# Two column blocks in one pass, splits ordered behind shifts, and stores moved to one queue, in a hybrid mixer and expert layer

## The chip, the cores and the metric

One core of a Trainium2 chip runs the whole layer. The metric is the device time of one execution in microseconds (us); lower is better. The engines are named as follows: TensorE (PE in the rows; PEld is its weight load), VectorE (DVE), ScalarE (ACT), GpSimd (POOL) and SyncE (SP, which here only issues DMAs).

## What is computed

One layer on 512 tokens of width 1024. A mixing sublayer projects x once, `p = h @ w_in`, and three mixers share the columns: trailing-window pooling, RWKV-7 (with a delta-rule state, and small "lora" projections for decay and gate), and a chunked mLSTM. Then an output projection, a norm, and an expert layer with 4 of 32 experts a token:

```python
p = h @ w_in[l]
y_pool, y_rwkv, y_mlstm = pool_mixer(p_pool), rwkv7_mixer(p_rwkv), mlstm_mixer(p_mlstm)
mix = jnp.concatenate([y_pool, y_rwkv, y_mlstm], axis=-1) @ w_out[l]
h = layer_norm(DEEPNORM_ALPHA * h + mix, ln1_g[l], ln1_b[l])
ffn = moe_ffn(h, router_w[l], router_b[l], w_gate_up[l], ...)
h = layer_norm(DEEPNORM_ALPHA * h + ffn, ln2_g[l], ln2_b[l])
```

In `rwkv7_mixer` the lora part is `w_log = -softplus(-(w0 + tanh(wd) @ w2)) - 0.5` and `g = sigmoid(gd) @ g2`, on columns that were first mixed with those of the token before (the token shift).

## The kernel before, in words

**Products in split form.** Every matmul of the mixing stage with x or a weight splits each operand into a high part (`xhi`, `whi`, made by ScalarE) and the rest (`xlo`, `wlo`, made by VectorE or GpSimd from the raw tile and the high part), lines 170 to 173. A product is then three matmuls: high by high, high by low, low by high (lines 222 to 224). x, transposed, comes as eight tiles of 128 x 512. A block of 128 columns of `w_in` comes as two tiles of 128 x 512 (four k each), through two raw buffers (`wraw`), four `whi` and four `wlo` (line 1590), so a raw buffer is free again when the low half has been made.

**The front.** `load_x` (183) loads x and the first block; `rwkv_lora` (511) takes the blocks of `ORDER` from the start: 1408 (decay and rate: `wdad`) and 1536 (gate: `gd`). `inproj_T` (213) takes a block from the queue of loaded ones, calls for the load of the next one, and does its 24 matmuls in a bank of tag `pi` (two banks; `ps` has four, `pm` two). `shift_mix` (505) evicts: ScalarE scales (507), VectorE adds the shifted columns (508). The tanhs follow (523, 525), and the lora matmul (566) needs the first of them. Then `rwkv_prep` runs k, r and v of the first heads, with transposes (`flip`, 606).

**The jam.** `rwkv_base` (674) inverts 32 x 32 blocks in a chain of 62 small VectorE operations (699, 701), whose result `xb` is stored to memory by four DMAs, two on SyncE, two on ScalarE (703), loaded back in another layout (704, `bb<-xd`) and transposed by VectorE (705). Beside this, TensorE does the mLSTM's v and o columns (`ml_vo`, 249 to 251), ScalarE evicts them (258, 259), and two last blocks of q and k follow (`ml_qk`, blocks 4 and 5, called "qk" below): evicted by 287, three taps on VectorE (289, `cv`), tanh 290, product 291 (`ks`). `rwkv_base_out` (712) places the blocks (`XT`, `X`: 728, 730, 733), with memsets on GpSimd (735); `rwkv_inv` (746) joins them to 128 x 128 inverses in steps over four chunks: 762 with puts 763, 768 with puts 769, 773 with X on ScalarE (774), 779, 784, 789. Score matmuls of the mLSTM (373) lie between. GpSimd works on `Vt` (844, 848), then makes the low halves of the `w_out` tiles, whose first four go through the same `wraw` buffers (`out_weights`, 869; load 877).

**Order.** The kernel is written in one order, and a scheduler orders the instructions of each engine from it before the run; each engine then runs its own list strictly in that order. `self.after(a, b)` only tells the scheduler to place a behind b.

## Time and profile before

| what | us |
|---|---|
| median of 3 runs (1463.05 to 1465.02) | 1463.57 |
| the profiled execution | 1465.28 |
| its span in the trace | 1463.5 |
| TensorE busy | 1334.6 (91%) |
| VectorE, ScalarE, GpSimd busy | 448.4, 289.5, 206.8 |
| DMA engines, mean rate over the span | 316 GB/s |

The page's rate by slices of 36.6 us goes from 253 GB/s in the first slice (x and the first weights) down to some 50 to 140 in the mixing stage, and from the twelfth slice on it stays near 400 until the end of the expert stage. The first matmul of the experts (line 1285) starts at 379.73. In a row of a timeline the first number is the start in us from the span's start, the second the length; "x5" groups neighbours; what stands in brackets is how long the engine had been idle and what released it. A released-by of "issue" names nothing that the trace shows; the engine's own queue is then where to look.

### The profile page before, as it was taken

The numbers are of one execution on the slowest core, as the hardware profiler recorded it, in microseconds if no ns is written. First come the engines' busy times: TensorE is split into PE (matmuls) and PEld (weight loads), VectorE is DVE, ScalarE is ACT, GpSimd is POOL, SyncE is SP. The second block draws the span as 40 slices with busy tenths as digits, with TensorE's granted clock in tenths as the row PEclk, the third lists the DMA queues.
The fourth block names the chain that finished last, engine by engine and source line by source line (L and its number), as shares of the span: only waits on it lengthen the run. The fifth ranks groups of instructions, "written<-read, shape, count | busy, mean of one in ns | idle before, by whom it ended". The sixth has DMA issues, their size and how long they took to land. (4 is left out here: it accounts for less than half of the span.)

```text
span 1463.5 us, 19946 instructions
## 1 busy us (share of the span) xinstructions
PE 1334.6 (91%) x7860; PEld 623.9 (43%) x7861; DVE 448.4 (31%) x1070; ACT 289.5 (20%) x617; POOL 206.8 (14%) x190
## 2 busy tenths in 40 slices
PE   7899978998999999987899999999879878899995
PEld 5677878876533333322233333333323222333323
DVE  5767687788521112111111121111111111211114
ACT  4444342453011111110001111111100100111103
POOL 1211236241001100110001111011100100010100
PEclk9999996899999999999999999999999999999998
DMA  7222233346899999999999999999999999999974
GB/s 253 73 58 72 52 79 99 132 141 269 297 364 375 396 385 403 396 390 395 403 403 397 396 398 399 406 394 394 391 389 402 394 404 395 400 395 415 408 297 118
DMA packets 95232, 461.88 MB, mean 316 GB/s; under 512 B 18084, under 2 KB 26692, under 8 KB 45962
## 3 DMA queue, kind: packets, MB, share of 16 engines
q1 hardware_dynamic: 79962, 435.61, 75.9%
q0 software_dynamic: 10592, 20.49, 6.5%
q10 hardware_dynamic: 4560, 4.15, 0.9%
q8 instruction: 82, 1.34, 0.4%
q14 instruction: 36, 0.29, 0.1%
HBM read 445.97 MB, written 18.10 MB: 317 GB/s over the span
## 5 line engine op out<-in xcount | busy, mean ns | idle before, releaser
L1285 PE MATMUL gu<-wc,xT 128*64 128x512 f32 x2048 | 486.5, 603 | 65.1 <-DMA wc<-w_gate_up 62.2
L1285 PEld LDWEIGHTS gu<-wc,xT 128*64 128x64 f32 x2048 | 143.1, 137 | 388.5 <-issue 243.1
L1298 DVE TENSOR_SCALAR glu<-gu 128x256 f32<-128x256 f32 (+1 forms) x64 | 35.6, 556 | 829.1 <-PE gu L1290 376.6
L1331 PE MATMUL dn<-wc,aT 128*64 128x512 f32 x1024 | 247.5, 603 | 4.2 <-PEq L1278 2.4
L1299 ACT ACTIVATE glu<-glu 128x256 f32<-128x256 f32 (+1 forms) x64 | 33.5, 524 | 543.1 <-DVE glu L1298 543.1
L1217 POOL DMA_INDIRECT xg<-hd,gidx x31 | 30.9, 998 | 670.8 <-PE tr L1230 660.8
L1331 PEld LDWEIGHTS dn<-wc,aT 128*64 128x64 f32 x1024 | 65.1, 136 | 118.9 <-issue 102.3
L1290 PE MATMUL gu<-wc,xT 128*32 128x512 f32 x960 | 111.5, 596 | 0.0
L1336 POOL DMA_INDIRECT yd<-eo,sidx x45 | 70.1, 1557 | 275.2 <-ACT eo L1335 275.2
L222 PE MATMUL pi<-xhi,whi 128*128 128x512 f32 x152 | 65.0, 428 | 15.9 <-ACT whi L172 8.9
L1231 ACT ACTIVATE xT<-tr 128x384 f32<-128x384 f32 x62 | 29.8, 490 | 181.1 <-PE tr L1230 181.1
L223 PE MATMUL pi<-xlo,whi 128*128 128x512 f32 x152 | 63.7, 419 | 0.5 <-DVE xlo L173 0.5
L224 PE MATMUL pi<-xhi,wlo 128*128 128x512 f32 x152 | 62.8, 413 | 0.0
L1290 PEld LDWEIGHTS gu<-wc,xT 128*32 128x32 f32 x960 | 27.0, 109 | 80.1 <-issue 79.8
L1335 ACT ACTIVATE eo<-dn,gate 128x512 f32<-128x512 f32 (+1 forms) x45 | 27.9, 621 | 163.0 <-PE dn L1331 88.9
L1326 PE MATMUL dn<-wc,aT 128*32 128x256 f32 x960 | 56.1, 381 | 1.0 <-ACT aT L1313 1.0
L173 POOL TENSOR_TENSOR wlo<-wraw,whi 128x512 fp32r<-128x512 f32 (+1 forms) x28 | 39.0, 1397 | 124.3 <-ACT whi L172 120.3
L1326 PEld LDWEIGHTS dn<-wc,aT 128*32 128x32 f32 x960 | 29.5, 110 | 34.0 <-issue 14.6
L172 ACT ACTIVATE whi<-wraw 128x512 fp32r<-128x512 f32 (+1 forms) x54 | 33.8, 634 | 47.8 <-DMA wraw<-w_in 21.9
L222 PEld LDWEIGHTS pi<-xhi,whi 128*128 128x128 f32 x152 | 30.0, 197 | 26.2 <-ACT whi L172 8.5
L1301 DVE SCALAR_TENSOR_TENSOR glu<-glu 128x256 f32<-128x256 f32 (+1 forms) x64 | 35.4, 555 | 7.2 <-ACT glu L1299 6.2
L1312 PEld LDWEIGHTS tr<-ident,glu 128*128 128x128 f32 x192 | 25.5, 208 | 26.4 <-DVE sel L1237 19.5
(489 smaller groups left out, 1501.1 us busy)
## 6 DMA issues: line engine op xcount, KB each, us to landing
wc<-w_gate_up SPq DMA_DIRECT2D x256, 1024.0 KB
wc<-w_down SPq DMA_DIRECT2D x128, 1024.0 KB
wraw<-w_in SPq DMA_DIRECT2D x46, 256.0 KB
wraw<-w_out SPq DMA_DIRECT2D x16, 256.0 KB
xraw<-xT SPq DMA_DIRECT2D x4, 512.0 KB
res<-x SPq DMA_DIRECT2D x4, 512.0 KB
hd<-res ACTq DMA_DIRECT2D x4, 512.0 KB
res<-yd POOLq DMA_DIRECT2D x4, 512.0 KB
```

The source lines that it names most:

```text
L172: self.hi_ins = nc.scalar.activation(hi, src, AF.Copy)
L173: return (eng or nc.vector).tensor_tensor(lo, src, hi, OP.subtract)
L222: nc.tensor.matmul(p, hi, xh, start=(k == 0), stop=False)
L223: nc.tensor.matmul(p, hi, xl, start=False, stop=False)
L224: nc.tensor.matmul(p, lo, xh, start=False, stop=(k == NK - 1))
L1285: mm(p[q][64 * h:64 * h + 64], xT[:, k, 0:64], w[:, 1024 * q + 512 * h:1024 * q + 512 * h + 512], start=False, stop=(k == NK - 1))
L1290: self.nc.tensor.matmul(p[2][32 * c:32 * c + 32], xT[:, k, 64:96], w4[:, c], start=False, stop=(k == NK - 1), skip_group_check=True)
L1298: nc.vector.tensor_scalar(out[:, c], g, 7.0, None, OP.min)
L1301: nc.vector.scalar_tensor_tensor(out[:, c], ln[:, c], 1.0, out[:, c], OP.add, OP.mult)
L1326: mm(p2[32 * c:32 * c + 32], aT[:, 4 + k % 2, 32 * (k // 2):32 * (k // 2) + 32], wd[k][:, 256 * c:256 * c + 256], start=(k == 0), stop=(k ...
L1331: mm(p0[64 * h:64 * h + 64], aT[:, k % 4, 64 * (k // 4):64 * (k // 4) + 64], wd[k][:, 512 * h:512 * h + 512], start=(k == 0), stop=(k == N ...
L1336: return nc.gpsimd.indirect_dma_start(out=self.yd.rearrange("t (c f) -> (t c) f", f=w), out_offset=bass.IndirectOffsetOnAxis(ap=self.sidx[ ...
```

## The change

It has these parts.

1. `load_x`: 20 matmuls on a zeroed tile (`idle`) into a bank of `pm` ahead of all others; the first two column blocks are loaded tile by tile between the tiles of x, first halves of both, then second halves (their low halves on VectorE; the second halves' raw buffers are those of the first).
2. `inproj_two`, new: both blocks in one pass over k, in banks of tag `ps` instead of `pi`. `rwkv_lora` calls it, shifts both, and only then loads the fourth block (the one behind the third, which `inproj_two` itself calls for), with its splits placed behind the scaling of the second shift. The tanhs come behind.
3. `rwkv_base`: the four stores of the inverted blocks are all issued by SyncE.
4. Three small casts of VectorE (`trib`, `sel0`) are placed behind the low half of the last of the first four tiles.

```diff
@@ -185,13 +185,39 @@
         self.xhi = [self.slot("x", f"xhi{q}", F32R)[:, :2048].rearrange("p (k t) -> p k t", k=4) for q in range(2)]
         self.xlo = [self.slot("yz"[q], f"xlo{q}", F32R)[:, :2048].rearrange("p (k t) -> p k t", k=4) for q in range(2)]
         xs = [self.slot("tu"[q], f"xraw{q}")[:, :2048].rearrange("p (k t) -> p k t", k=4) for q in range(2)]
-        for q in range(0, NK, 2):
-            nc.sync.dma_start(xs[q // 4][:, q % 4:q % 4 + 2], self.a["xT"][128 * q:128 * q + 256].rearrange("(k p) t -> p k t", p=128))
-            if q == 0:
-                self.wq, self.at = deque(), 0
-                self.load_next()
-        for k in range(NK):
-            self.split(xs[k // 4][:, k % 4], self.xhi[k // 4][:, k % 4], self.xlo[k // 4][:, k % 4], nc.gpsimd if k in (3, 6) else None)
+        z = self.slot("k", "idle", BF)[:, 0:512]
+        nc.vector.memset(z, 0.0)
+        p = self.bank("pm")
+        for _ in range(20):
+            nc.tensor.matmul(p, z[:, 0:128], z, start=True, stop=True)
+        x2 = lambda k, n: nc.sync.dma_start(xs[k // 4][:, k % 4:k % 4 + n], self.a["xT"][128 * k:128 * (k + n)].rearrange("(k p) t -> p k t", p=128))
+        sx = lambda k: self.split(xs[k // 4][:, k % 4], self.xhi[k // 4][:, k % 4], self.xlo[k // 4][:, k % 4], nc.gpsimd if k in (3, 6) else None)
+        self.wq, self.at, w, self.w_ins = deque(), 2, [[], []], []
+
+        def load(b, q):
+            raw, hi, lo = self.wtiles(4, 128)
+            c0 = ORDER[b][0]
+            nc.sync.dma_start(raw, self.a["w_in"][:, NK * c0:NK * (c0 + 128)].rearrange("p (k c) -> p k c", k=NK)[:, q:q + 4])
+            w[b] += [(hi[:, k], lo[:, k]) for k in range(4)]
+            return raw, hi, lo
+
+        x2(0, 1)
+        w0 = load(0, 0)
+        x2(1, 1)
+        w1 = load(1, 0)
+        for k in (2, 4, 6):
+            x2(k, 2)
+        sx(0)
+        self.split(*w0)
+        sx(1)
+        self.split(*w1)
+        sx(2)
+        sx(3)
+        self.split(*load(0, 4))
+        self.start_lo = self.split(*load(1, 4))
+        for k in range(4, NK):
+            sx(k)
+        self.wq.extend((ORDER[b][0], w[b]) for b in range(2))
 
     def load_w(self, c0, n, m, eng=None):
         src = self.a["w_in"][:, NK * c0:NK * (c0 + n)].rearrange("p (k c) -> p k c", k=NK)
@@ -200,6 +226,7 @@
             raw, hi, lo = self.wtiles(m, n)
             self.nc.sync.dma_start(raw, src[:, q:q + m])
             self.split(raw, hi, lo, eng)
+            self.w_ins.append(self.hi_ins)
             out += [(hi[:, k], lo[:, k]) for k in range(m)]
         return out
 
@@ -223,6 +250,20 @@
             nc.tensor.matmul(p, hi, xl, start=False, stop=False)
             nc.tensor.matmul(p, lo, xh, start=False, stop=(k == NK - 1))
         return p
+
+
+    def inproj_two(self):
+        nc = self.nc
+        w = [self.wq.popleft()[1] for _ in range(2)]
+        self.load_next()
+        ps = [self.bank("ps") for _ in range(2)]
+        for k in range(NK):
+            xh, xl = self.xhi[k // 4][:, k % 4], self.xlo[k // 4][:, k % 4]
+            for p, (hi, lo) in zip(ps, (z[k] for z in w)):
+                nc.tensor.matmul(p, hi, xh, start=(k == 0), stop=False)
+                nc.tensor.matmul(p, hi, xl, start=False, stop=False)
+                nc.tensor.matmul(p, lo, xh, start=False, stop=(k == NK - 1))
+        return ps
 
 
     def ml_vo(self):
@@ -519,9 +560,14 @@
         self.one = self.sp.tile([128, 4, 129], BF, name="one")
         nc.gpsimd.memset(self.one, 1.0)
         nc.gpsimd.memset(self.one[:, :, 0:1], 0.0)
-        self.after(self.shift_mix(self.inproj_T(1408), 9, self.wdad), self.hi_ins)
+        p0, p1 = self.inproj_two()
+        self.shift_mix(p0, 9, self.wdad)
+        first = self.shift_mix(p1, 10, self.gd)
+        self.w_ins = []
+        self.load_next()
+        for d in self.w_ins:
+            self.after(d, first)
         nc.scalar.activation(self.wdad[0:64], self.wdad[0:64], AF.Tanh)
-        self.shift_mix(self.inproj_T(1536), 10, self.gd)
         nc.scalar.activation(self.gd, self.gd, AF.Tanh, scale=0.5)
         nc.vector.tensor_scalar(self.gd, self.gd, 0.5, 0.5, OP.mult, OP.add)
         sr = [self.slot("r", f"R{q}") for q in range(2)]
@@ -700,7 +746,7 @@
                                     mb[:, t, t + 1:].unsqueeze(1).to_broadcast([96, t + 1, 31 - t]), OP.mult)
             nc.vector.tensor_tensor(xb[:, 0:t + 1, t + 1:], xb[:, 0:t + 1, t + 1:], v, OP.add)
         for q in range(4):
-            (nc.scalar if q % 2 else nc.sync).dma_start(quad(xd)[q], xb[24 * q:24 * q + 24])
+            nc.sync.dma_start(quad(xd)[q], xb[24 * q:24 * q + 24])
         nc.sync.dma_start(xtc, xd)
         nc.vector.transpose(sb[:, 1280:2048], sb[:, 512:1280])
         self.base_out, self.ys = (xtc, xc), sb[:, 0:512]
@@ -1152,7 +1198,7 @@
         self.onesb = self.cp.tile([128, 128], BF, name="onesb")
         nc.gpsimd.memset(self.onesb, 1.0)
         self.trib = self.cp.tile([128, 128], BF, name="trib")
-        nc.vector.tensor_copy(self.trib, c["mask2"][:, 0:128])
+        self.after(nc.vector.tensor_copy(self.trib, c["mask2"][:, 0:128]), self.start_lo)
         self.mkb = self.cp.tile([128, NT, NE], BF, name="mkb")
         self.sel0 = self.expert_sel(0)
         self.ro = self.cp.tile([128, 3, NT, 4], F32, name="ro")
@@ -1233,8 +1279,12 @@
 
     def expert_sel(self, e):
         sel = self.mw.tile([128, 2, 128], F32R, name="sel") if e else self.cp.tile([128, 2, 128], F32R, name="sel0")
-        self.nc.vector.tensor_scalar(sel[:, 0], self.c["bsel0"], 2.0 * e, None, OP.is_equal)
-        self.nc.vector.tensor_scalar(sel[:, 1], self.c["bsel2"], 4.0 * e, None, OP.is_equal)
+        d = self.nc.vector.tensor_scalar(sel[:, 0], self.c["bsel0"], 2.0 * e, None, OP.is_equal)
+        if not e:
+            self.after(d, self.start_lo)
+        d = self.nc.vector.tensor_scalar(sel[:, 1], self.c["bsel2"], 4.0 * e, None, OP.is_equal)
+        if not e:
+            self.after(d, self.start_lo)
         return sel
 
 
```

Where the instructions go, at three places. The same statements have later line numbers in the changed kernel: 258 is 299 there, 287 is 328, 703 is 749, 774 is 820.

ScalarE at the end of v and o, before; `whi<-wraw` is the split of a `w_in` tile, V and so are the evictions:

```order
L256 ACTIVATE V_1543<-ps 128x4x64 x2
L172 ACTIVATE whi<-wraw 128x512 x2
L703 DMA xd<-ba 24x32x32 x2
L258 ACTIVATE V_1543<-pi 128x2x64
L259 ACTIVATE so<-pi 128x128
L258 ACTIVATE V_1543<-pi 128x2x64
L259 ACTIVATE so<-pi 128x128
L258 ACTIVATE V_1543<-pm 128x2x64
L259 ACTIVATE so<-pm 128x128
```

And now:

```order
L297 ACTIVATE V_1591<-ps 128x4x64 x2
L172 ACTIVATE whi<-wraw 128x512 x3
L299 ACTIVATE V_1591<-pi 128x2x64
L300 ACTIVATE so<-pi 128x128
L172 ACTIVATE whi<-wraw 128x512
L299 ACTIVATE V_1591<-pi 128x2x64
L300 ACTIVATE so<-pi 128x128
L299 ACTIVATE V_1591<-pm 128x2x64
L300 ACTIVATE so<-pm 128x128
```

The two stores are gone from this list; the next block's first tile is split ahead of the first eviction, and its second between the first and second pair of evictions.

ScalarE later, at the inverse, before; the `whi` here are those of the `w_out` tiles:

```order
L730 ACTIVATE XT<-bb 32x12x32 x4
L287 ACTIVATE cv<-pi,pcol 128x512
L172 ACTIVATE whi<-wraw 128x512 x2
L774 ACTIVATE X<-ps 32x6x32 x4
L903 ACTIVATE mr<-Y 128x128
L903 ACTIVATE mr<-lora 128x128
L172 ACTIVATE whi<-wraw 128x512 x2
L290 ACTIVATE cv<-cv 128x512
```

And now:

```order
L328 ACTIVATE cv<-pi,pcol 128x512
L776 ACTIVATE XT<-bb 32x12x32 x4
L331 ACTIVATE cv<-cv 128x512
L172 ACTIVATE whi<-wraw 128x512 x3
L820 ACTIVATE X<-ps 32x6x32
L172 ACTIVATE whi<-wraw 128x512
L820 ACTIVATE X<-ps 32x6x32 x3
L949 ACTIVATE mr<-Y 128x128
```

The third `w_out` tile's split now stands ahead of the first X, the fourth's ahead of the second; block five's tanh (290, now 331) has moved from behind all of them to ahead.

VectorE around the transpose of the inverted blocks, before:

```order
L173 TENSOR_TENSOR wlo<-wraw,whi 128x512
L705 STREAM_TRANSPOSE bb<-bb 128x768
L173 TENSOR_TENSOR wlo<-wraw,whi 128x512
L341 COPY cdec<-pm 128x12
L346 COPY Q<-pm 128x96
L289 SCALAR_TENSOR_TENSOR cv<-pi,pcol,cv 128x511
L289 SCALAR_TENSOR_TENSOR cv<-pi,pcol,cv 128x510
L289 SCALAR_TENSOR_TENSOR cv<-pi,pcol,cv 128x509
L728 COPY XT<-bb 32x12x32
```

And now:

```order
L382 COPY cdec<-pm 128x12
L387 COPY Q<-pm 128x96
L330 SCALAR_TENSOR_TENSOR cv<-pi,pcol,cv 128x511
L330 SCALAR_TENSOR_TENSOR cv<-pi,pcol,cv 128x510
L330 SCALAR_TENSOR_TENSOR cv<-pi,pcol,cv 128x509
L764 MEMSET X 32x24x32
L332 SCALAR_TENSOR_TENSOR ks<-cv 128x512
L330 SCALAR_TENSOR_TENSOR cv<-pi,pcol,cv 128x511
L330 SCALAR_TENSOR_TENSOR cv<-pi,pcol,cv 128x510
L330 SCALAR_TENSOR_TENSOR cv<-pi,pcol,cv 128x509
L751 STREAM_TRANSPOSE bb<-bb 128x768
L774 COPY XT<-bb 32x12x32
```

The three `cv` operations of block five have come ahead of the transpose, which were spread over the puts of line 780 before; the `ks` of block four too.

At the front, the first tanh now stands behind the two splits of block four on ScalarE, and the lora matmul (566, now 612) on TensorE behind 11 of the third block's 24 matmuls (ahead of all of them before). The flip of v (606, now 652) comes 5 matmuls later in the block that it interrupts.

## Rows read from the trace of the kernel before

**Rows 1.** Busy time, clock, DMA share, GB/s of a stretch: the expert stage.
```profile
380.00:1410.00 1030.00, 960.23 (x5470) 330.50 (x5466) 144.71 (x338) 116.19 (x236) 100.05 (x76) 1.00 1.01 393
```

**Rows 2.** Timeline, TensorE, front (start, duration, operation, [idle <- released by]).
```profile
15.16 0.45 PE L224 MATMUL pi<-xhi,wlo 128*128 128x512 f32 x1
...
23.60 0.40 PE L224 MATMUL pi<-xhi,wlo 128*128 128x512 f32 x1
23.93 1.13 PE L566 MATMUL ps<-lora 64*128 64x512 f32 x4
...
46.64 0.65 PE L606 MATMUL ps<-ident,M 128*128 128x128 f32 x4 [0.98 <-DVE M L508]
```

**Rows 3.** Timeline, VectorE, front.
```profile
11.28 5.28 DVE L173 TENSOR_TENSOR xlo<-xraw,xhi 128x512 fp32r<-128x512 f32 x5
```

**Rows 4.** Timeline, ScalarE, front.
```profile
19.95 0.63 ACT L523 ACTIVATE lora<-lora 64x512 f32<-64x512 f32 x1 [0.82 <-DVE lora L508]
20.97 0.63 ACT L172 ACTIVATE whi<-wraw 128x512 fp32r<-128x512 f32 x1 [0.40 <-DMA wraw<-w_in]
```

**Rows 5.** Timeline, ScalarE, jam.
```profile
213.76 1.02 ACTq L703 DMA_DIRECT2D xd<-ba  x2
214.83 0.28 ACT L258 ACTIVATE V<-pi 128x128 f32<-128x128 f32 x1 [6.22 <-issue]
...
238.91 0.32 ACT L774 ACTIVATE X<-ps 32x192 f32<-32x192 f32 x1 [5.39 <-PE ps L773]
...
242.99 0.32 ACT L774 ACTIVATE X<-ps 32x192 f32<-32x192 f32 x1 [1.04 <-PE ps L773]
...
245.28 0.63 ACT L172 ACTIVATE whi<-wraw 128x512 fp32r<-128x512 f32 x1 [0.76 <-DMA wraw<-w_out]
```

**Rows 6.** Timeline, TensorE, jam.
```profile
215.33 0.80 PE L222 MATMUL pi<-xhi,whi 128*128 128x512 f32 x1 [7.04 <-ACT so L259]
...
229.14 0.39 PE L224 MATMUL pi<-xhi,wlo 128*128 128x512 f32 x1
...
235.04 0.79 PE L373 MATMUL pi<-qs,ks 64*128 64x128 f32 x2 [3.77 <-DVE ks L291]
...
243.34 5.06 PE L779 MATMUL ps<-X,M 64*64 64x64 f32 x45
...
250.84 1.22 PE L373 MATMUL pi<-qs,ks 64*128 64x128 f32 x4
...
255.45 6.82 PE L789 MATMUL ps<-R,XT 128*128 128x128 f32 x35
```

**Rows 7.** Busy times by stretch (next to last three: clock, DMA share, GB/s).
```profile
214.00:216.00 2.00, 0.67 (x2) 0.57 (x3) 0.86 (x2) 1.17 (x8) 0.21 (x1) 0.50 0.67 134
```

**Rows 8.** Timeline, SyncE's queue (DMA issues).
```profile
18.23 1.03 SPq L201 DMA_DIRECT2D wraw<-w_in  x2
...
240.57 7.04 SPq L877 DMA_DIRECT2D wraw<-w_out  x4
```

**Rows 9.** Timeline, VectorE, jam.
```profile
208.44 0.68 DVE L173 TENSOR_TENSOR wlo<-wraw,whi 128x512 fp32r<-128x512 f32 x1
...
225.33 2.30 DVE L289 SCALAR_TENSOR_TENSOR cv<-pi,pcol,cv 128x511 f32<-128x511 f32 x3
227.55 0.81 DVE L728 COPY XT<-bb 32x384 f32<-32x384 f32 x1
228.47 0.70 DVE L718 MEMSET X<- 32x768 f32 x1
...
233.62 1.37 DVE L291 SCALAR_TENSOR_TENSOR ks<-cv 128x512 f32<-128x512 f32 x1
235.02 1.52 DVE L763 COPY X<-ps 32x192 f32<-32x192 f32 x4
```

**Rows 10.** Timeline, GpSimd, jam.
```profile
229.65 1.92 POOL L735 MEMSET XT<- 32x384 f32 x3 [0.93 <-PE pi L224]
...
239.28 2.48 POOL L173 TENSOR_TENSOR wlo<-wraw,whi 128x512 fp32r<-128x512 f32 x2
```

## The prediction

> **What bounds the kernel now.** I read the busy times by stretch first. From 380 to 1410 us the DMA engines are busy all the time, at 393 GB/s [rows 1]: the expert stage streams its weights. It begins when the mixing stage is over, so an edit of the mixing stage alone moves the end by what it moves that start; I take this as one for one. The change sits at two places there, and I then read both in the timeline, engine by engine.
>
> *The front, to 47 us.* TensorE starts 36 intervals between the matmuls at 15.16 and 23.60, 0.234 us each, which is the upper clock level [rows 2]. Before that VectorE sets the pace: it makes the low halves one behind the other, five of x taking 5.28 us from 11.28 up to 16.56 [rows 3]. The tanh of the first block runs at 19.95, long before the lora matmul at 23.93 needs it [rows 2, 4]. At 46.64 TensorE lost 0.98 us to the shift of v on VectorE [rows 2].
>
> *The jam, 208 to 256 us.* ScalarE wants to evict V and so, but two stores of the inverted blocks stand ahead in its queue and wait for the chain on VectorE to end; they go at 213.76 and the first eviction starts at 214.83 after 6.22 us idle [rows 5]. TensorE stands still until 215.33 [rows 6], and the granted clock is 0.50 in 214 to 216, the lower level [rows 7]. Then qk block four, block five (last matmul 229.14), the copies of the inverse, and a wait of 3.77 us at 235.04 for ks [rows 6].
>
> **The change, part by part.** *Warm-up matmuls.* Twenty on zeroed data, in a time when TensorE waits for x anyway: cost nothing; what covers them is the wait of the first real matmul for the first splits.
>
> *Two blocks together.* Both want k = 0 to 3 while the splits still run, so TensorE works inside VectorE's time. VectorE's list is x as before to 16.5, then two more w low halves at about 0.6: 17.7. What is left, k = 4 to 7 of both, is 24 matmuls, 24 x 0.234 = 5.6, and the first of them can run from 16.7: end 22.3, against 23.60 + 0.23 = 23.83 before. Gain 1.5.
>
> *Fourth block's splits behind the shifts.* The tanhs now stand on ScalarE behind two splits that wait for tiles. Before, a tile issued at 18.23 [rows 8] was split at 20.97 [rows 4]: 2.7 us. The tiles of block four can be issued only when the low halves of block three are done, about 21.4 and 22.2; they land near 24 and 25, the second split ends at 25.6, the tanh at 26.2. The lora matmul stands after 11 matmuls of block three, reached at 22.3 + 2.6 = 24.9: stall 1.3. It gives back nearly all of the 1.5: net -0.2. Five more matmuls ahead of the flip of v cover up to 0.98 of the wait at 46.64. Front: **-0.5**, ends -1.5 and +1.
>
> *All stores on SyncE.* ScalarE was idle from 208.6 (214.83 less 6.22). But block five's first split now stands ahead of the first eviction, its second ahead of the rest. The tile is issued when VectorE is through with a low half of block four, made from 208.44 for 0.68 [rows 9] and now one operation of the chain (0.35) earlier: 208.8. It lands at 211.5, split to 212.15; V and so follow; TensorE restarts at 212.6, 2.7 earlier, after 4.3 us idle instead of 7.04. If the clock holds, 24 x 0.234 makes block four end at 218.2 and block five at 224.2 instead of 229.4. SyncE issues two stores more, 1.02 as ScalarE's two took [rows 5], so the load of the inverted blocks is about that later; no matter, since ahead of the transpose now stand the second block's three cv operations, 2.30 together as the first block's [rows 9]. 224.4 + 0.8 + 2.3 = 227.5, transpose 228.4, copies of 5.4 us (227.55 to 235.02, less the memset of 0.70 and ks of 1.37, which now stand elsewhere), so the first put comes at 233.8 instead of 235.02 [rows 9]: **1.2 earlier**. The puts are then no longer interrupted by ks, and the first X could be evicted at about 236.6.
>
> *What is late next.* That X. In ScalarE's new order the splits of the third and fourth w_out tiles stand ahead of the first and the second X; before, all four X came first, from 238.91 on, and the fourth tile's split at 245.28 after a wait for its load [rows 5]. There are two raw buffers, so the third load waits until GpSimd has made the first w_out low half, the fourth for the second. GpSimd made these two from 239.28, 2.48 long, and SyncE issued the loads from 240.57 [rows 8, 10]. GpSimd works without a gap from the memsets at 229.65, which waited 0.93 for qk block five [rows 10]. In the change that wait goes, and its earlier work begins some 0.7 sooner (V of the first tokens early, the other three behind block five's second split, at about 215): 1.6 earlier. So the low halves end at 238.9 and 240.2 instead of 240.5 and 241.76. Loads take 2.7 (above) to 3.5 (241.76 to 245.28); I take 3.1. Fourth tile's split 243.3 to 243.9, second X gone at 244.2. Behind it are four groups of six small matmuls: 18 of them took 1.36 (four X from 238.91 to 242.99, three intervals), so 1.8: the next stage, at 243.34 before [rows 6], starts at **246.0, 2.7 later** (0.6 of a us either way by the load). Four of the six score matmuls between there and 255.45 are moved away (1.22 at 250.84 [rows 6]): -1.3 with what they hold up. Jam: **+1.4**.
>
> Ends for the jam: if GpSimd were 3 us earlier than I think, X comes as it is ready, and -3; if GpSimd is no earlier and loads take 3.5, the stage starts 4.7 later, so +3.4.
>
> The Trainium skill ("TensorE: Matmul & The Clock Gate", Part 1) says the low clock is the default and that an idle stretch brings it back. By that, block four could start at the lower level after its 4.3 us; no row of this kernel shows so short a stop ahead of large matmuls. The sum would stay, since X waits for the tile until 242 in either case, and rival 3 below would come out at 1462 instead of 1460.4.
>
> *Small ones.* The mask and selector copies moved behind the splits (0.6 together) lie on VectorE's idle time from 16.6; nothing.
>
> **Sum.** -0.5 + 1.4 = +0.9. The profiled execution took 1465.28, so 1466.2; it lies 1.7 above the median of the runs (1463.57), so **1464.5**, which is no change: 0.2%, about what a measurement of this kernel can tell from none, is 2.9 us.
>
> **The rivals.**
> 1. *No change, as summed* (chance 0.5): 1462 to 1466.4. For it: both places win at first and each has a new wait close behind.
> 2. *GpSimd late, so slower* (0.22). ScalarE's X waits for the tile, the tile for GpSimd. If evictions of V behind block five's second tile leave GpSimd where it was (low halves done at 240.5 and 241.76), the second X is at 245.9, the stage 4.7 later; less 1.3 and 0.5 this is +2.9, and 1466.5 or, with the lora stall 1 us longer, 1467.5. It decides at the end of the second w_out low half: after 241.7 slower, before 240 not. Against it: the 0.93 wait surely goes.
> 3. *The tiles are there in time* (0.23). Then the puts and copies set the pace: X at 236.6, the stage starts about 2.2 to 3 earlier: -2.6 - 0.5, from 1463.57 it is 1460.4, and 1459 if the front keeps more. For it: GpSimd's order changes too, and its work may pack more tightly than I think. Against it: it must gain 4 us more.
> 4. *The change doesn't do what it says* (0.05): the stores were not what held TensorE; some other wait takes over at 215 and 1463.6 stays.
>
> **How the numbers follow.** Faster than 1460.64: most of rival 3 and a little of the first, 0.24. Slower than 1466.5: most of rival 2 and the edge of the first, 0.23. Rest 0.53. The range reaches from 1459.5 to 1467.4; the likeliest case alone is 1462 to 1466.4.
>
> **What would show it.** Front: both blocks' last matmul near 22.3, a wait of about 1.3 us before the lora matmul, on ScalarE. Jam: TensorE restarts near 212.6; transpose near 227.5; ScalarE idle ahead of the third w_out split, released by a load, then X at 242 to 244; the stage after it near 246. Wrong, if X is evicted before 239 or the lora matmul does not wait. The expert stage should begin within 1 us of where it did.

## The result and the profile after

| | kernel before | changed kernel |
|---|---|---|
| first comparison, median | 1465.02 (7 runs) | 1473.92 (7 runs), ratio 1.0053 [1.0034, 1.0073] |
| second comparison (run e9 below) | 1464.42 (35 runs) | 1470.79 (12 runs), ratio 1.0041 [1.0022, 1.0060] |
| the profiled execution | 1465.28, span 1463.5 | 1469.0, span 1467.2 |
| first matmul of the experts | 379.73 | 384.76 |

The change makes the kernel **slower**, by 6 to 9 us; the prediction said no change, 1464.5, with a range up to 1467.4. In the profiled execution the expert stage begins 5.0 us later and the span is 3.7 longer, since the expert stage itself took 1.3 less. This execution is the fastest of the seven; what the others lose beyond it stands in no trace. I go through the two places in the order of the prediction.

**The front.** The timeline of TensorE in the changed kernel, 14 to 48 us, only the two rows that waited (start, length, engine, line, operation, and in brackets the idle time before and what ended it):

```profile
25.32 1.13 PE L612 MATMUL ps<-lora 64*128 64x512 f32 x4 [1.62 <-ACT lora L570]
47.21 0.66 PE L652 MATMUL ps<-ident,M 128*128 128x128 f32 x4 [1.54 <-DVE M L549]
```

The same stretch of ScalarE, the splits of the fourth block and the first tanh behind them:

```profile
23.46 1.29 ACT L172 ACTIVATE whi<-wraw 128x512 fp32r<-128x512 f32 x2 [1.60 <-DMA wraw<-w_in]
24.65 0.61 ACT L570 ACTIVATE lora<-lora 64x512 f32<-64x512 f32 x1
```

This is as forecast: the tanh stands behind splits that wait for their tile, and the lora matmul waits 1.62 for it and starts at 25.32, against 23.93 [rows 2]. The wait for v at 46.64 [rows 2] did not go; it is 1.54 now, at 47.21, and the next one grew too, to 1.71 at 52.83 (0.70 at 50.78 before). The first matmul of the pooling mixer starts at 58.20, 58.43 before, so the front keeps 0.2 there. The inversion chain on VectorE begins 0.2 later than before all the same (175.88, 175.69): nothing of it reaches the jam.

**The chain.** Not looked at in the prediction: the stretch between front and jam. VectorE's timeline, 176 to 216 us, at the start of the chain, and its end:

```profile
176.81 0.25 DVE L745 TENSOR_TENSOR bb<-ba 96x87 f32<-96x87 f32 x1
179.46 0.73 DVE L332 SCALAR_TENSOR_TENSOR ks<-cv 128x512 f32<-128x512 f32 x1 [2.40 <-ACT cv L331]
...
215.63 0.21 DVE L747 TENSOR_TENSOR ba<-ba,bb 96x31 f32<-96x31 f32 x1
```

The product `ks` of an earlier qk block (index 3, called block three below) now stands inside the chain and waits 2.40 for its tanh on ScalarE. The chain ends at 215.84 instead of 213.73. Its last row in the kernel before:

```profile
213.52 0.21 DVE L701 TENSOR_TENSOR ba<-ba,bb 96x31 f32<-96x31 f32 x1
```

**The jam, ScalarE and TensorE.** ScalarE's rows that answer to [rows 5]:

```profile
213.59 0.63 ACT L172 ACTIVATE whi<-wraw 128x512 fp32r<-128x512 f32 x1 [3.22 <-DMA wraw<-w_in]
...
243.18 0.63 ACT L172 ACTIVATE whi<-wraw 128x512 fp32r<-128x512 f32 x1 [9.03 <-DMA wraw<-w_out]
244.33 0.32 ACT L820 ACTIVATE X<-ps 32x192 f32<-32x192 f32 x1 [0.51 <-PE ps L819]
```

TensorE's, answering to [rows 6]: block four's first three matmuls, block five's last, and the first step of the inverse:

```profile
214.60 0.80 PE L249 MATMUL pi<-xhi,whi 128*128 128x512 f32 x1 [4.62 <-ACT so L300]
215.19 0.63 PE L250 MATMUL pi<-xlo,whi 128*128 128x512 f32 x1
215.62 0.63 PE L251 MATMUL pi<-xhi,wlo 128*128 128x512 f32 x1
...
228.84 0.39 PE L251 MATMUL pi<-xhi,wlo 128*128 128x512 f32 x1
...
241.18 2.04 PE L808 MATMUL ps<-bb,M 32*32 32x32 f32 x45 [6.03 <-DVE X L809]
```

And the granted clock behind the restart, from the windows (stretch, us, TensorE busy, PEclk, DMA share, GB/s):

```profile
216.00:218.00 2.00, 2.00 (x6) 0.50 0.48 72
218.00:220.00 2.00, 2.00 (x6) 0.50 0.82 123
220.00:222.00 2.00, 2.00 (x10) 0.92 0.88 246
```

TensorE restarts at 214.60, not at 212.6. Up to 220 its clock is at the lower level, 0.50, and a matmul starts every 0.43 us (215.19 to 215.62) instead of every 0.234. Block five's last matmul starts at 228.84, 229.14 before [rows 6]: of the 0.73 by which TensorE restarted earlier, 0.30 is left.

**The jam, VectorE.** The rows that answer to [rows 9]: block five's taps, the transpose behind them, three copies of X, the first put:

```profile
230.08 2.31 DVE L330 SCALAR_TENSOR_TENSOR cv<-pi,pcol,cv 128x511 f32<-128x511 f32 x3 [2.17 <-ACT cv L328]
232.31 0.97 DVE L751 STREAM_TRANSPOSE bb<-bb 128x768 f32<-128x768 f32 x1
...
233.80 2.94 DVE L779 COPY X<-bb 32x384 f32<-32x384 f32 x3
...
240.78 1.52 DVE L809 COPY X<-ps 32x192 f32<-32x192 f32 x4
```

GpSimd in the same time, answering to [rows 10]:

```profile
229.36 1.65 POOL L781 MEMSET XT<- 32x384 f32 x3 [0.34 <-PE pi L251]
...
232.66 2.07 POOL L894 TENSOR_TENSOR Vt<-Vt,lora 128x384 f32<-128x384 f32 x2
...
239.16 2.71 POOL L173 TENSOR_TENSOR wlo<-wraw,whi 128x512 fp32r<-128x512 f32 x2
```

The transpose runs at 232.31. In the kernel before it ran at 223.18, as soon as its load had come; block four's taps stood behind it, block five's much later (243.83). From its end to the first put 7.5 us pass with copies, three of X taking 2.94 together. In the kernel before three took 1.22, at a time when GpSimd stood still at first (until 229.65 [rows 10]). The two rows of before:

```profile
223.18 0.98 DVE L705 STREAM_TRANSPOSE bb<-bb 128x768 f32<-128x768 f32 x1 [2.62 <-DMA bb<-xd]
...
229.09 1.22 DVE L733 COPY X<-bb 32x384 f32<-32x384 f32 x3
```

One copy by itself, from narrower windows of the timeline: first in the changed kernel, with GpSimd's add that ran beside it (234.0 to 234.6), then in the kernel before, with GpSimd idle (229.2 to 229.35):

```profile
233.62 1.11 POOL L894 TENSOR_TENSOR Vt<-Vt,lora 128x384 f32<-128x384 f32 x1
233.80 1.14 DVE L779 COPY X<-bb 32x384 f32<-32x384 f32 x1
...
229.09 0.28 DVE L733 COPY X<-bb 32x384 f32<-32x384 f32 x1
```

The first copy ends at 234.94, 0.21 after the add (234.73). So it is in every profile here: of the 152 copies of X and XT in the 19 profiles, 139 begin while a GpSimd instruction runs, and each of them ends 0.21 to 0.26 us after that instruction does; they took 0.31 to 1.33 us. The six with no GpSimd instruction beside them took 0.28 to 0.35.

SyncE in the changed kernel, and its load in the kernel before:

```profile
215.87 2.60 SPq L749 DMA_DIRECT2D xd<-ba  x4
...
220.70 0.33 SPq L750 DMA_DIRECT2D bb<-xd  x1
...
218.98 0.34 SPq L704 DMA_DIRECT2D bb<-xd  x1
```

The load of the inverted blocks goes out 4.9 after the chain's end (220.70 less 215.84); before it was 5.25 (218.98 less 213.73). So here four stores on one queue made the way through memory no longer. (In e2 and e16 below it goes out 6.5 after the chain's end; two w_out loads issued ahead of it take SyncE 3.5 there, 1.27 here.) The first put comes at 240.78 (235.02), the stage behind X at 248.76 (243.34 [rows 6]), 5.4 later.

### The profile page after: what moved, and what is told of

Its sections match the earlier page's. It is cut to its first block, busy times and chain, and to the rows that moved or that the text cites. A ratio compares the mean times of both kernels' runs of the same rounds, so it can differ in the third digit from the quotient of the medians.

```text
span 1467.2 us, 19991 instructions
## 1 busy us (share of the span) xinstructions
PE 1338.2 (91%) x7880; PEld 626.7 (43%) x7881; DVE 447.9 (31%) x1071; ACT 289.0 (20%) x617; POOL 207.2 (14%) x190
## 5 line engine op out<-in xcount | busy, mean ns | idle before, releaser
L1348 DVE TENSOR_SCALAR glu<-gu 128x256 f32<-128x256 f32 (+1 forms) x64 | 35.6, 556 | 830.6 <-PE gu L1340 379.3
L249 PE MATMUL pi<-xhi,whi 128*128 128x512 f32 x136 | 57.9, 426 | 4.6 <-ACT so L300 4.6
L251 PE MATMUL pi<-xhi,wlo 128*128 128x512 f32 x136 | 56.4, 415 | 0.0
L250 PE MATMUL pi<-xlo,whi 128*128 128x512 f32 x136 | 56.3, 414 | 0.0
L1376 PEld LDWEIGHTS dn<-wc,aT 128*32 128x32 f32 x960 | 29.6, 110 | 33.9 <-issue 14.6
L1350 DVE TENSOR_SCALAR glu<-gu 128x256 f32<-128x256 f32 (+1 forms) x64 | 35.2, 551 | 2.8 <-PE gu L1335 2.8
```

Of the source, the lines that this page charges most:

```text
L249: nc.tensor.matmul(p, hi, xh, start=(k == 0), stop=False)
L250: nc.tensor.matmul(p, hi, xl, start=False, stop=False)
L251: nc.tensor.matmul(p, lo, xh, start=False, stop=(k == NK - 1))
L1348: nc.vector.tensor_scalar(out[:, c], g, 7.0, None, OP.min)
L1350: nc.vector.tensor_scalar(ln[:, c], l, 7.0, -7.0, OP.min, OP.max)
L1376: mm(p2[32 * c:32 * c + 32], aT[:, 4 + k % 2, 32 * (k // 2):32 * (k // 2) + 32], wd[k][:, 256 * c:256 * c + 256], start=(k == 0), stop=(k ...
```

## Experiments

In the tables, "chain" is the time from the first to the last start in the inversion chain, and "transpose", "put", "stage" and "solve" are the starts of the transpose, the first put, the stage behind X and the first matmul with R, all counted from the chain's end in the profile of that run, since the chain ends at other times in each. Ratios are to the kernel before, on the same chip, with the 95% interval.

### The parts apart

Two kernels: the change with the old stores (two issued by SyncE, two by ScalarE), and the kernel before with only the new ones.

```diff
e1, e10 (from the changed kernel)
-            nc.sync.dma_start(quad(xd)[q], xb[24 * q:24 * q + 24])
+            (nc.scalar if q % 2 else nc.sync).dma_start(quad(xd)[q], xb[24 * q:24 * q + 24])
e2 (from the kernel before): the opposite
```

e1:


> All of the change but the stores, which go from two queues again. Theory A (two faults of order, each its own: the ks product of the third qk-side block, index 3, stands in the chain of the block inverse and waits about 2.4 us for its tanh; and the transpose stands behind block five's taps): here only the first fault is left. A wait for ScalarE of 2 to 3 us in the first steps of the chain, chain end near 215.8 (213.7 before), transpose near 225, expert stage 1 to 2.5 us later than the 379.7 of before. Rival B (the front is harmless or gains, all loss comes from the stores): chain end at 213.7 or earlier, expert stage at 379.7 or up to 0.8 earlier. Rival C (it is the granted clock, not the order): order shows no wait, time differs only with the mean clock.

e2:


> The kernel before with only the four stores moved to SyncE. Theory A: no wait in the chain (end 213.7 as before), but the transpose now stands behind two of block five's three taps: near 228 to 230 instead of 223.2, the step after X (243.3 before) at 246 to 248, expert stage 2.5 to 4.5 us later. Rival B says the same, and that this is all of the loss: expert stage 5 us later. Rival D (X waits for the third w_out tile, as I predicted): ScalarE idle on that tile's load right up to the first X, X at 242 to 244, and the step after it at 246, whatever the transpose does.

e10, e1 once more:


> The change without the moved stores, once more, since the first run of it was faster (0.9975) and the same with block three's ks later was not (0.9990). If the front parts gain by themselves: 1462 to 1464, ratio 0.997 to 0.9985. If the first run had luck with the clock: 1465 to 1467, ratio 0.999 to 1.0005.

e9, the changed kernel once more on e10's chip:


> The changed kernel itself once more, on the same chip as the next three, since its seven runs so far had a lower mean granted clock (0.965 to 0.975) than most others. Theory (the order of the work costs it): 1470 to 1475, ratio 1.003 to 1.006. Rival (those seven runs had bad luck with the clock): under 1469, ratio under 1.002.

| run | median | ratio | chain | transpose | put | stage | solve |
|---|---|---|---|---|---|---|---|
| before | | 1 | 37.8 | 9.5 | 21.3 | 29.6 | 41.7 |
| changed | 1473.92 | 1.0053 [1.0034, 1.0073] | 39.8 | 16.5 | 24.9 | 32.9 | 44.3 |
| e9, the same | 1470.79 | 1.0041 [1.0022, 1.0060] | 39.8 | 16.5 | 25.0 | 33.0 | 44.3 |
| e2 stores alone | 1472.32 | 1.0031 [1.0015, 1.0046] | 37.8 | 14.9 | 23.4 | 33.3 | 46.0 |
| e1 without stores | 1462.49 | 0.9975 [0.9961, 0.9990] | 39.8 | 8.5 | 20.1 | 28.4 | 40.6 |
| e10, the same | 1465.50 | 0.9996 [0.9975, 1.0017] | 41.9 | 8.7 | 18.8 | 27.5 | 39.6 |

The loss comes with the moved stores: alone they make the kernel slower, and without them it is not slower. What the rest gives by itself is small: two runs of one kernel gave 0.9975 and 0.9996. The long chain, on the other hand, is there in e1 and not in e2, so block three's `ks` was put into it by the front parts. (In the profiles of e10 and e7 below, the chain is longer still; the granted clock was 0.50 for 17 us ahead of and in its start, and that this is why is not shown.) VectorE in e2 shows what the stores did:

```profile
227.38 1.53 DVE L289 SCALAR_TENSOR_TENSOR cv<-pi,pcol,cv 128x511 f32<-128x511 f32 x2 [1.99 <-ACT cv L287]
228.83 0.97 DVE L705 STREAM_TRANSPOSE bb<-bb 128x768 f32<-128x768 f32 x1
```

Here too the transpose stands behind taps of block five, which wait for ScalarE's eviction of that block.

### The order of VectorE's work

Four edits of the changed kernel that only tell the scheduler to place one instruction behind another: block three's `ks` behind the ninth step of the chain (e3), block five's taps behind the transpose (e11), both (e4, and once more e15), and the third and fourth w_out split behind all four X (e7 alone, e5 with both others).

```diff
-            nc.vector.scalar_tensor_tensor((self.q2 if j < 3 else self.k2)[j % 3], th, 1.0, x, OP.add, OP.mult)
+            d = nc.vector.scalar_tensor_tensor((self.q2 if j < 3 else self.k2)[j % 3], th, 1.0, x, OP.add, OP.mult)
+            if j == 3:
+                self.after(d, self.chain[8])
...
+                if j == 5 and s == 1:
+                    self.after(d, self.tr_ins)
...
-            self.after(self.hi_ins, self.xt_ins)
+            self.after(self.hi_ins, self.xt_ins if n < 2 else self.xl_ins)
```

e3:


> The changed kernel with one more order rule: the ks product of block index 3 behind the ninth step of the chain. Theory A: the 2.4 us wait goes, chain end 213.2 to 213.7, and all of the jam is 1.7 to 2.4 us earlier than in the changed kernel: transpose near 230, the step after X near 246.5 (248.8), expert stage near 382.5 (384.8). Rival B: no change against the changed kernel beyond 0.5 us at the expert stage, since the transpose waits for block five's taps and these for TensorE.

e11:


> The changed kernel with only the transpose of the inverted blocks ahead of block five's taps; the wait of block three's ks in the chain stays. Theory (two wrong places in VectorE's order, each costing a part): transpose near 226.5, first put near 234, 1465 to 1468. Rival (the w_out tiles set the pace, so the transpose does not matter): the stage after X starts as late as in the changed kernel, near 248, and 1470 to 1474. If only the ks wait mattered (the run with ks later gave 1467): 1471 or more.

e4:


> As e3, and block five's taps ordered behind the transpose. Theory A: transpose at 224 to 227, first put at 231.5 to 234, step after X at 240 to 243.5, expert stage 377 to 380, time within 0.2% of the kernel before or a little below. Rival D (tile): the step after X no earlier than 246, expert stage 382 or later, because the third and fourth w_out splits still stand ahead of X. Rival C: the mean clock stays below that of the kernel before and the time above it by 0.4% whatever the order.

e15:


> The changed kernel with ks of block three later and the transpose ahead of block five's taps, once more, since it had the best ratio to the kernel before (0.9979). If it is faster than the kernel before: 0.997 to 0.999 again. If that run had luck with the clock: 0.9995 to 1.001.

e7:


> The changed kernel with only the third and fourth w_out splits ordered behind the four X. My prediction's step (the jam is set by that tile) would have it 2 us or more faster than the changed kernel, step after X at 246.5 or earlier. Theory A (the transpose sets X there, the tile's split ended 0.5 us before X was ready): step after X at 248 to 248.8, time that of the changed kernel within 1 us, so 0.4 to 0.6% above the kernel before.

e5:


> As e4, and the third and fourth w_out splits ordered behind all four X. Theory D (in e4 the second X waited for the tile: idle on the load up to 241.9, VectorE 5.39 behind it): the wait goes, X at about 234.8, 236.2, 237.5, 238.9, step after X at 239.5 (244.4 in e4), expert stage 3 to 5 us earlier than e4's 376.2 if nothing else fills it, median 1457 to 1460. Rival E: the 5 us come back later, since in e4 they were made up again between the R step and the expert stage (VectorE's chain there, and w_out now later): expert stage 375 to 376.5, median within 1 us of e4.

| run | median | ratio | chain | transpose | put | stage | solve |
|---|---|---|---|---|---|---|---|
| e3 ks later | 1467.16 | 1.0008 [0.9991, 1.0024] | 38.5 | 15.4 | 23.4 | 31.9 | 43.3 |
| e11 transpose first | 1463.67 | 0.9996 [0.9976, 1.0016] | 39.8 | 11.9 | 18.5 | 32.1 | 44.4 |
| e4 both | 1462.65 | 0.9979 [0.9965, 0.9993] | 38.5 | 11.4 | 18.3 | 31.5 | 43.8 |
| e15, the same | 1463.26 | 0.9992 [0.9972, 1.0011] | 38.4 | 11.5 | 18.2 | 31.6 | 43.9 |
| e7 X first alone | 1471.27 | 1.0029 [1.0011, 1.0046] | 41.8 | 15.9 | 24.6 | 33.0 | 44.3 |
| e5 all three | 1463.95 | 0.9985 [0.9968, 1.0001] | 38.4 | 11.2 | 17.1 | 25.4 | 37.5 |

The transpose's place alone takes the whole loss away (e11; the changed kernel on the same chip had 1.0041), and e3 most of it; both together (e4) take away no more than e11. By what way is not shown by the profiles. In e11 the put comes 6.5 earlier than in e9, counted from the chain's end, but the solve does not (44.4 against 44.3), since X now waits for its tile there, as in e4 below; what is shorter is the time from the solve to the experts, 120.7 against 124.6, with 14.6 us at the lower clock level against 21.5. In e3 the transpose is late still (15.4). Putting X ahead of the w_out splits, where the prediction saw the limit, leaves the kernel slow (e7). VectorE in e11, the transpose and the first put:

```profile
228.29 0.95 DVE L753 STREAM_TRANSPOSE bb<-bb 128x768 f32<-128x768 f32 x1
...
234.89 1.52 DVE L811 COPY X<-ps 32x192 f32<-32x192 f32 x4
```

Once the transpose is early, the wait that the prediction named does appear. ScalarE in e4:

```profile
234.82 0.32 ACT L825 ACTIVATE X<-ps 32x192 f32<-32x192 f32 x1 [5.55 <-PE ps L824]
240.04 0.63 ACT L172 ACTIVATE whi<-wraw 128x512 fp32r<-128x512 f32 x1 [4.91 <-DMA wraw<-w_out]
241.26 0.63 ACT L172 ACTIVATE whi<-wraw 128x512 fp32r<-128x512 f32 x1 [0.59 <-DMA wraw<-w_out]
241.92 0.54 ACT L825 ACTIVATE X<-ps 32x192 f32<-32x192 f32 x2
```

The first X goes at 234.82 and the second at 241.92, behind two splits that wait for their loads. e5 takes this away: the stage behind X begins 25.4 after the chain instead of 31.5, and the solve 37.5 instead of 43.8. The time does not follow: 0.9985 against 0.9979 and 0.9992.

### Where six microseconds of the jam go

From the solve to the first expert matmul e4 and e15 take 119.4 and 120.2 us, e5 125.8, the changed kernel 124.7 and 124.6, the kernel before 124.3. I summed, for the 19 profiles of this study, how long the granted clock was 0.50 in that stretch. It goes from 9.6 us (e4) to 24.7 (e2), and the length follows it: the line through the 19 points is 115 us and 0.48 us for each us at the lower level, correlation 0.93. Two of the profiles, by windows of 4 us, the changed kernel first:

```profile
270.00:274.00 4.00, 3.27 (x26) 1.00 0.22 89
274.00:278.00 4.00, 2.85 (x13) 0.62 0.75 250
278.00:282.00 4.00, 4.00 (x18) 0.50 0.01 3
```

and e11:

```profile
270.00:274.00 4.00, 3.18 (x27) 1.00 0.61 245
274.00:278.00 4.00, 3.59 (x32) 1.00 0.25 86
278.00:282.00 4.00, 4.00 (x34) 1.00 0.15 52
```

Both stop shortly in the chain over chunks there (0.73 us idle against 0.82 in 270 to 274, 1.15 against 0.41 in 274 to 278), and in the first the clock falls, from about 275 to 289. The kernel before stops there for longer (2.6 us at one place) and fell for only 3.4 in its profile. So this fall is not set by the change in any way that these runs show; it is the larger part of what differs between the profiles in this stretch.

The whole executions leave a rival open. The mean granted clock over a kernel's runs is 0.970 to 0.974 in each of the seven kernels with a late put (more than 23 us behind the chain's end), and 0.973 to 0.978 in the others; e9 has 0.972, e11 0.976. With two levels, 0.0042 less clock (0.9722 against 0.9764) is 0.0084 of the span, 12 us, more at the lower level in e9. At 0.29 us for each (the slope between executions of one kernel, over all runs) to the 0.48 from above, this is an estimate of 4 to 6 us of the 7.1 between their medians. So the order may cost by its waits, or by a lower clock that goes with it; no run parts the two.

One try at the clock itself: e12 is e5 with twelve matmuls of no use ahead of block four, on constants, into a bank whose content is no longer needed.

```diff
+            if q == 0:
+                self.busy = ps[0]
...
+            if j == 4:
+                for _ in range(12):
+                    nc.tensor.matmul(self.busy, self.one[:, 0, 0:128], self.one[:, :, 1:129], start=True, stop=True)
             p = self.inproj_T(1664 + 128 * j)
```

> The best order so far (ks later, transpose ahead of the taps, X ahead of the third and fourth w_out split) with 12 matmuls of no use in TensorE's 4.6 us stop ahead of block four, whose results nobody reads; the orders of the other engines stay as they were. If the stop is what brings the lower clock level: the granted clock of the 6 us after the restart is 0.9 or more and block four takes 5.6 us instead of 8; the end moves by 0 to -1.5 only (1462.5 to 1464), since the transposed blocks, not block five, set the first put there. If the level falls for another reason: block four as before, 1464.

Measured 1463.67, 0.9991 [0.9972, 1.0009]. The stop was cut to 2.06, and the lower level came all the same. TensorE, and its windows:

```profile
215.78 0.69 PE L249 MATMUL pi<-xhi,whi 128*128 128x512 f32 x1 [2.06 <-ACT so L302]
```

```profile
216.00:218.00 2.00, 2.00 (x6) 0.50 0.46 132
218.00:220.00 2.00, 2.00 (x8) 0.67 0.78 117
```

A stop filled up to the restart was not tried.

### The stores by themselves

Is there a cost of the moved stores that no order mends? First try: e13 (stores alone, with e7's rule) and e14 (whole change, with e3's and e7's rules) hold block four's first tap behind the transpose. So e14 is e5 but for the block that is held back, four instead of five.

```diff
+                if j == 4 and s == 1:
+                    self.after(d, self.tr_ins)
```

e13:


> The kernel before with only the stores moved to SyncE, and with the old order put back where it mattered: the transpose ahead of the second block's third tap at the latest, all four X ahead of the third and fourth w_out split. If only the order costs: transpose near 223, the stage after X at 239 to 242, and 1462 to 1466 (ratio 0.998 to 1.001, against 1.0031 for the stores alone). If the moved stores cost by themselves: transpose 11 us or more behind the chain's end and 1468 or more (1.002 and up).

e14:


> The whole change with ks of block three behind the ninth step of the chain, the transpose ahead of block five's taps (and not held for longer), X ahead of the third and fourth w_out split. If the copies and puts set the pace of the jam once the order is mended: the stage after X starts 25 us or less behind the chain's end (29.8 before, 33.1 in the changed kernel), and 1461 to 1464 (0.997 to 0.999). If what is gained there is lost again behind it: 1465 to 1467.

Both missed: 1472.59, 1.0042 [1.0027, 1.0057], and 1470.77, 1.0045 [1.0024, 1.0067]. VectorE in e13:

```profile
228.60 1.53 DVE L289 SCALAR_TENSOR_TENSOR cv<-pi,pcol,cv 128x511 f32<-128x511 f32 x2 [2.72 <-ACT cv L287]
230.05 0.97 DVE L707 STREAM_TRANSPOSE bb<-bb 128x768 f32<-128x768 f32 x1
...
239.25 0.75 DVE L289 SCALAR_TENSOR_TENSOR cv<-pi,pcol,cv 128x511 f32<-128x511 f32 x1
240.03 0.35 DVE L765 COPY X<-ps 32x192 f32<-32x192 f32 x1
```

With block four's taps held back, the scheduler set block five's in their place, ahead of the transpose, and block four's among the puts. The edit made what it was to remove. It is one more pair of kernels with a late transpose (15.4 and 15.3 after the chain) and a late put (25.4 and 24.6), and both are slow. Second try, e16 (stores alone, with e7's rule) and e17 (whole change, with e3's and e7's): both blocks' taps behind the transpose (`put_ins` is the transpose here), and the memset of X behind it and behind block four's last tap.

```diff
+                if j >= 4 and s == 1:
+                    self.after(d, self.tr_ins if j == 4 else self.put_ins)
+                if j == 4 and s == 3:
+                    self.after(self.xc_ins, d)
...
+        self.xc_ins = nc.vector.memset(x24[:, :, 32:64], 0.0)
+        self.after(self.xc_ins, self.m_ins)
+        self.after(self.xc_ins, self.tr_ins)
+        self.put_ins = self.tr_ins
```

e16:


> The kernel before with only the stores on SyncE, and the transpose ahead of the taps of both blocks and of the memset of X, X ahead of the third w_out split but for one. If the place of the transpose is the whole loss of the stores alone (1.0031): transpose 8 to 10.5 us behind the chain's end (15.1 there, 9.7 in the kernel before), first put 20 or less behind it (23.6 and 21.5), 1461 to 1465, ratio 0.997 to 1.000. If the moved stores cost by themselves: 1.002 or more although the transpose is early.

e17:


> The whole change with the same rules and ks of block three behind the ninth step of the chain. If the place of the transpose decides: first put 20 us or less behind the chain's end, ratio 0.997 to 0.9995. If what is won in the jam is lost again behind it, or the parts of the front cost: 1.000 to 1.002.

```profile
224.57 0.98 DVE L709 STREAM_TRANSPOSE bb<-bb 128x768 f32<-128x768 f32 x1 [2.70 <-DMA bb<-xd]
...
231.38 0.35 DVE L770 COPY X<-ps 32x192 f32<-32x192 f32 x1
```

In e16 (above) the transpose waits for its load again, 10.2 after the chain, and the put comes 17.0 after it. 1466.81, 1.0002 [0.9986, 1.0018], where the stores alone had 1.0031: so with another order their loss is gone. That the stores by themselves neither cost nor give is not shown, since this order has an earlier put than the kernel before (17.0, 21.3) and the old stores were not run with it. e17: transpose 8.7, put 15.7, 1465.24, 1.0000 [0.9981, 1.0018]; a gain was expected, and the earliest put of all gave none.

### Two smaller ones

e6 is e1 with `ks` of block three later, e8 is e1 without the rule that sets the fourth block's splits behind the second shift.

```diff
e8
-        self.w_ins = []
         self.load_next()
-        for d in self.w_ins:
-            self.after(d, first)
```

e6:


> The change without the moved stores and with the ks product out of the start of the chain: what the front parts are worth alone. Theory A: chain end 212.7 to 213.4 (216.7 with the wait in e1), transpose at 222 to 223, step after X at 242 to 243, expert stage 376.5 to 378.5, median 1 to 3 us under e1. Rival F (e1's gain is the granted clock of its later stages, not the front, and the wait for ks was covered): median equal to e1 within 1 us.

e8:


> e1 without the rule that puts the fourth block's splits behind the shifts: the first of them then stands ahead of the shifts on ScalarE, the second still ahead of the tanhs. If the rule matters as I costed it (the tanh waits for the tiles either way), the lora matmul is at 25.5 to 28 against 25.25 with it, and the time within 0.1% of e1. If holding the shift back behind a tile costs more, the lora matmul goes to 27 or later and the chain begins 0.5 to 1.5 us later than e1's 176.7.

e6: 1465.52, 0.9990 [0.9974, 1.0007], chain 38.4 instead of 39.8; no gain over e1 is seen, and in its profile the time from the solve to the experts is 127.8, of it 24.0 at the lower clock level. e8: 1466.23, 1.0005 [0.9986, 1.0024]; the lora matmul starts at 26.85 instead of 25.25 in e1, since a split of the fourth block that waited 3.68 for its tile now stood ahead of both shifts. In the 14 profiles of kernels with the rule it starts at 24.92 to 26.25, so the rule does give some 0.6 to 1.9 us at that place.

## Why the prediction was wrong

**The front: right in its number.** Forecast -0.5 with a lora wait of 1.3; measured -0.2 at the pooling mixer with a wait of 1.62. Both blocks were through at 20.97, earlier than my 22.3, but two waits behind took it back, 1.54 for v, where I had counted on five more matmuls to cover it, and the 1.71 at 52.83. So the number came out by two misses of opposite sign, which is luck in part, and at the start of the chain nothing is left of it (0.2 later).

**What was missed altogether: +2.0.** The prediction took the chain to end when it did, less one operation. The change also moved block three's `ks` into it, where it waits 2.40; with it later (e3) the chain takes 38.5, of 39.8 here and 37.8 before. A look at the order between the two places would have shown it. By it the tile of block five, whose issue waits for a low half made inside the chain, is late, and with it "TensorE restarts at 212.6": it was 214.60.

**"If the clock holds": +3.0.** The prediction counted 24 x 0.234 for block four and named the other case beside it. TensorE stood still 4.62 and came back at the lower level; 214.60 to 228.84 and 0.39 is 14.6 for what was to take 11.6. By the rule that the prediction set beside its sum (the Trainium skill, "TensorE: Matmul & The Clock Gate", Part 1: the low clock is the default and idleness brings it back), this was to be expected, and the trace agrees: 0.50 up to 220. The prediction's sentence that the sum would stay even so was the mistake, for it held only as long as X waited for the tile. Its words that no row shows so short a stop ahead of large matmuls were wrong, too. The kernel before has one, of 2.29, and the lower level behind it:

```profile
69.60 1.85 PE L499 MATMUL pm<-pbd 128*128 128x512 f32 x2 [2.29 <-DVE pbd L496]
```

```profile
70.00:73.00 3.00, 3.00 (x7) 0.50 0.01 3
```

This stop of 2.29 stands in all 19 profiles; in 14 the clock fell behind it, in 5 it did not.

**"Copies of 5.4 us": +2.1.** They took 7.5, since GpSimd's adds on `Vt` run at the same time and a copy ends only behind the add beside it; three copies of X took 2.94, against 1.22. The Trainium skill, "SBUF — State Buffer", "Who interferes with whom", says that a copy of VectorE in a two-port fast mode and a GpSimd instruction lock each other out. The trace agrees: all 139 copies that began beside a GpSimd instruction ended 0.21 to 0.26 behind it. That these copies are in such a mode no row shows.

These three make 7.1; the first put came 7.0 later than the "233.8" of the prediction, at 240.78 (the sum went on from 224.4 where it had 224.2).

**"What is late next. That X": not in this kernel.** X waited 0.51 for TensorE and not for a tile, and the stage behind it began at 248.76, not 246.0, because the puts were late. The wait for the third and fourth tile was real but second: it stood behind the puts, and came to light when those were mended (e4: 4.91 on the load; e5 without it: the stage 6.1 earlier from the chain's end). So the jam came out at +5.4 for the stage behind X where I had 2.7, and nothing was made good behind it: 5.0 at the experts. The four score matmuls that I took off, 1.3, gave 0.8 at most: the solve, at 255.45 before [rows 6], starts at 260.10, 4.65 later.

**The rivals.** Slower was given 0.22, by GpSimd being late with the tiles. Its sign came true: the second low half ended at 241.87 (239.16 and 2.71), past the 241.7 that the prediction set, and 0.1 later than before where the sum had GpSimd 1.6 earlier. So that term failed as well. But the loss did not come that way: the third tile was split by 243.81, 0.5 ahead of the first X, and no X waited for a tile.

**What the runs settle.** In the 7 profiles with the put more than 23 us behind the chain's end the ratios go from 1.0008 to 1.0053; in the 12 with an earlier one, the kernel before among them, from 0.9975 to 1.0005. In two pairs only the order around the transpose differs, and their intervals stand clear of each other: e11 and e9, e5 and e14. So the order there costs the loss, and the moved stores brought it. What stays open is the way from the late transpose to the later end (e11's solve is no earlier than e9's), why e3 gains without it, and why the later stretch takes back what e5, e16 and e17 gain in the jam: all this goes with the granted clock, but no run held that clock still.

## What to carry to other kernels

Moving an instruction from one queue to another frees what stood behind it, and the scheduler then makes another order on engines that the edit does not name: read the whole new order between the edit and the end of its stage, and look for an operation that waits for a late producer ahead of one that the next stage needs. When work starts earlier after a stop, price it at the lower clock level as well. Where copies of VectorE move next to other work, look at what GpSimd does at that time. And a rule that holds one operation back can put a worse one in its place, so hold the wanted one ahead of all its rivals, and look again.

## Unexpected of the hardware

After stops of 4.62 us and, in e12, of 2.06 us TensorE worked at the lower level, 0.50 in 216 to 218; in the changed kernel its large matmuls were then 0.43 instead of 0.234 us apart. Behind one and the same stop of 2.29 us the clock fell in 14 profiles and not in 5. In the stretch behind the solve it fell for 3.4 to 13.7 us or not at all, around stops of 0.8 to 2.8 us: for 3.4 and not at all in the two profiles of e4's kernel, for 13.7 and 13.6 in those of the changed one. At 0.48 us for each us of it, this moves single executions by several us, and it may be a part of why two medians of 12 runs of one kernel, on two chips, stand at 0.9975 and 0.9996. A copy of VectorE that begins while a GpSimd instruction runs ended 0.21 to 0.26 us behind it, 139 times of 139: copies of 0.28 to 0.35 us took up to 1.33.
